# Attention scores as 64-row products, with both softmax maps of a head issued together

## The chip, the cores and the metric

The kernel runs on one core of one Trainium2 chip. The metric is the device time of one execution in microseconds, the median of several runs. Below, PE is the matrix engine (TensorE), PEld its loading of weights, DVE the vector engine, ACT the scalar engine, POOL GpSimd and SP the engine that issues most DMAs.

## The reference, cut to what matters

One layer of a decoder takes 1024 prompt tokens and 8 x 4 sample tokens of width 1024. One input projection feeds a differential attention branch (4 heads) and a state space branch; one output projection adds both to the residual. In the attention, queries and keys are RMS-normed over 64 elements, and each head has two softmax maps:

```python
q = _rmsnorm(q.reshape(b, L, N_HEADS, 2, QK_DIM), q_g)     # QK_DIM = 64
k = _rmsnorm(k.reshape(b, L, N_HEADS, 2, QK_DIM), k_g)
s = jnp.einsum('bqhcd,bkhcd->bhcqk', q, k) * (QK_DIM ** -0.5)   # c: the two maps
s = jnp.where(mask, s + bias, NEG_INF)
p = jax.nn.softmax(s, axis=-1)
w = p[:, :, 0] - lam * p[:, :, 1]
o = jnp.einsum('bhqk,bkhe->bqhe', w, v)
```

The keys (normed) and values of all tokens are outputs too.

## The kernel before, in words

The program has three stages. In the first (about 0 to 240 us) the tokens are loaded and transposed, and the state space branch runs; the order of its PE work is written out by hand. In the second (about 240 to 546 us) `project` computes, head by head and for two tiles of 128 tokens at a time (j = 0 to 3), the head's queries, keys, values and gate. In the third (to the end) `finish` loads the earlier outputs and computes the output projection. The attention of a head (`attention`) runs beside the second and third stage.

In the second and third stage the order is made in two steps. `mix` (line 228) advances several generators in turn: projection, prompt attention and sample attention. Each `yield` names a planned duration, and each stream gets a share of the planned clock. This gives the order of the program text. The tile framework then places each engine's instructions: of those whose inputs and buffers are ready by its own estimate, it takes the one that stands first in the text. So an instruction that isn't ready is passed by later ones, and on the chip each engine runs the order so made.

Float32 operands are split in a high and a low part of type float32r, and products are sums of such parts. In the projections a product is high x high + high x low + low x high, accumulated in one bank of PSUM (`acc`, three buffers).

The part that is changed is this. `keep_qkv` (lines 887 to 912) takes the normed queries and keys of two tiles of tokens, transposes them on PE (line 895, into a buffer `tr`), and writes them to a tile `pt` of 1536 columns. On the 128 partitions the first 64 belong to map 0, the others to map 1. For each map c the high parts of the queries (line 904, ACT) are copied to the other 64 partitions (line 905, DVE), the low parts (line 906, DVE) likewise (line 907, DVE), and the keys of the map get their high parts on partitions 0 to 63 (line 908, ACT) and their low parts on partitions 64 to 127 (line 909, DVE). So one product over all 128 rows gives q x (k high + k low). The keys in float32 (line 910, ACT, tile `kf`) go to the output by a DMA.

`scores` (lines 981 to 1029) handles one block of 128 queries (qb = 0 to 7) against the 128 (qb + 1) keys before it. For each map it goes through segments of up to 512 keys; a segment has one PSUM buffer `sc`, of which there are two. For each 256 keys there are two products (high queries, low queries; lines 1006 and 1007), each with 128 x 128 weights. DVE then reads the segment, adds the bias and takes the minimum (line 1018, one or two instructions to a segment), which frees the buffer. ACT takes the exponential of a map (line 1023), DVE joins both maps (line 1028), and `values` transposes the weights (line 1043) and multiplies them with the values (`pv`). A head has 12 segments to a map. `attn_norm` and `attn_out` (lines 1057 to 1089) norm the result (line 1072, tile `o`) and transpose it (line 1079); the last head's result is written where its queries were in `pt`.

All matrix products go through a helper, line 134, so in the profile they are told apart by their tiles: `acc<-ws,xt` (projection of prompt tokens), `acc<-ws,xs` (of sample tokens, 64 columns of weights), `acc<-ws,o` and `acc<-ws,pt` (output projection), `sc<-pt` (scores), `sc<-cached,qz` (scores of sample tokens, 32 columns of weights), `tr<-cn,qn` (transposes; 32 rows for the sample tokens).

Of the kernel before, what the change touches and what calls it, by code (L numbers as in the profile page):

```python
# [40 lines left out]
# The first phase in its order on the tensor engine: a letter per kind of step, then its index.  # L41
UNITS = ("M0 T0 C20 D0 U0 L0 W N0 M1 P0 C30 X U1 L1 C21 C32 S0 N1 C31 C22 U2 L2 O0 M2 G G U3 S1 G N2 L3 G O1 "
         "M3 G P1 G S2 N3 Q0 G G S3 Z1 G A0 G O2 Z0 B0 Z2 O3 H0 Z3 H1 G H2 G Y0 H3 Y1 Y2 Y3").split()
# Lags of steps of the heads in microseconds, shares of the streams, priorities, numbers of buffers.
# [81 lines left out]
class Kernel:  # L126
# [37 lines left out]
    def load_w(self, src, nk, more=0):  # L164
        """more: the first ones go to tiles of the last phase."""
        nc = self.nc
        w = []
        for kt in range(nk):
            raw = self.raws.tile([128, W], F32, name="wraw", tag="wraw", bufs=3)
            s = src(kt)  # L170
            nc.sync.dma_start(raw.rearrange("p (s c) -> p s c", s=s.shape[1]) if len(s.shape) == 3 else raw, s)
            w.append(self.split_w(raw, kt < more))
        return w
# [11 lines left out]
    def stream_b(self, c0, first=0):  # L185
        """The columns c0.. in halves: a tile holds 256 columns of two row blocks."""
        nc, src = self.nc, self.I["w_in"]
        for half in range(first, 2):
            for k2 in range(KT // 2):
                raw = self.raws.tile([128, W], F32, name="wraw", tag="wraw", bufs=3)  # L190
                c = c0 + 256 * half
                nc.sync.dma_start(raw.rearrange("p (k c) -> p k c", k=2),
                                  src[256 * k2:256 * k2 + 256, c:c + 256].rearrange("(k p) c -> p k c", k=2))
                yield self.split_w(raw)
# [33 lines left out]
    def mix(self, *lanes, until=False):  # L228
        """Emits the pieces of several streams, each getting its share of time; None is a stream that has to wait.
        until: to the end of the first stream only."""  # L230
        lanes = [[g, share, 0.0] for g, share in lanes]
        main = lanes[0]
        while main in lanes if until else lanes:
            for lane in sorted(lanes, key=lambda l: l[2]):
                x = next(lane[0], -1)
                if x == -1:
                    lanes.remove(lane)
                    break
                if x is not None:
                    lane[2] += x / lane[1]  # L240
                    self.clock += x
                    break
            else:
                self.clock += 0.3
            for lane in lanes:
                lane[2] = max(lane[2], main[2] - CAP)
# [9 lines left out]
    def load_x(self, g):  # L256
        """Three tiles of tokens, transposed, as a sum of two parts; their squares summed."""
# [124 lines left out]
    def gate(self, w):  # L382
        """A quarter of twice a silu(): the other gate's tanh() + 1 is twice a sigmoid, too."""
# [52 lines left out]
    # Gate of the state space branch  # L436
# [30 lines left out]
    def glu(self, mo):  # L467
# [5 lines left out]
        # the first one starts before the last inputs are there  # L473
# [27 lines left out]
    def ssm_tables(self):  # L501
# [52 lines left out]
        # the powers of all groups, once for the real and once for the imaginary parts  # L554
# [65 lines left out]
    def ssm_maps(self, m):  # L620
# [4 lines left out]
        # input map of one chunk, states on columns  # L625
# [17 lines left out]
        # output map, real parts of the state above imaginary ones  # L643
# [19 lines left out]
    def ssm_kernel(self, m):  # L663
# [9 lines left out]
        # kernel of one chunk  # L673
# [16 lines left out]
    def ssm_states(self, m):  # L690
# [15 lines left out]
        # recurrence over chunks, turned back by the phase  # L706
# [56 lines left out]
    def lam(self):  # L763
# [18 lines left out]
        # relative bias, negated, over distances  # L782
# [6 lines left out]
    def bias(self):  # L789
# [13 lines left out]
        # of the sample group's rows (batch % 4, -, batch / 4, map, query): distances of the last keys  # L803
        self.bias_rows = lambda h: bass.AP(tensor=d.tensor, offset=row(h) + 127, ap=[[0, 32], [VW, 4], [1, 132]])

    def start_heads(self):
        nc = self.nc
        # one batch's queries, or weights, on the columns of its rows, zeros elsewhere
# [8 lines left out]
    def pt(self, name, dt=F32R):  # L817
        return self.att.tile([128, 1536], dt, name=name, tag="pt", bufs=6)
# [21 lines left out]
    def project(self, w):  # L840
        """The heads' columns for all tokens, into self.heads."""
        nc = self.nc
        due = self.due
        for h in range(NH):
            st = {"ga": {}, "PT": {}, "V": {}, "kept": {}, "out": set()}
            self.heads.append(st)
            for j in range(4):
# [3 lines left out]
                # the last two side by side, so that the weights' tiles get free one after the other  # L851
# [29 lines left out]
    def silu(self, out, x, half_r):  # L881
        """out half_r = silu(2 half_r x)"""
        e = self.small("silu", 128)[0:out.shape[0]]
        self.nc.scalar.activation(e, x, AF.Tanh, scale=half_r)
        self.nc.vector.scalar_tensor_tensor(out, e, 1.0, x, op0=OP.add, op1=OP.mult)

    def keep_qkv(self, h, j, qn, vo, st):
# [10 lines left out]
        half = [slice(64 * c, 64 * c + 64) for c in range(2)]  # L898
        with self.tc.high_priority(HP2):
            # queries of a map twice, one above the other; keys' high parts above their low parts  # L900
            for c, ps in enumerate(half):
                hi, lo, kk = (pt[:, 512 * z + 256 * c:512 * z + 256 * c + 256] for z in range(3))
                ot = half[1 - c]
                nc.scalar.activation(hi[ps], q[ps], AF.Copy, scale=self.gains[ps, 0:1])
                v.tensor_copy(hi[ot], hi[ps].bitcast(F32))  # L905
                v.scalar_tensor_tensor(lo[ps], q[ps], self.gains[ps, 0:1], hi[ps].bitcast(F32), op0=OP.mult, op1=OP.subtract)  # L906
                v.tensor_copy(lo[ot], lo[ps].bitcast(F32))
                nc.scalar.activation(kk[half[0]], k[ps], AF.Copy, scale=self.pkc("k_g")[ps])
                v.scalar_tensor_tensor(kk[half[1]], k[ps], self.pkc("k_g")[ps], kk[half[0]].bitcast(F32), op0=OP.mult, op1=OP.subtract)  # L909
            nc.scalar.activation(kf, k, AF.Copy, scale=self.pkc("k_g"))  # L910
# [19 lines left out]
    def mm_sample(self, a, x, w, kts):  # L930
        """The sample tokens' products, of the high parts in rows 0.. and of the low parts in rows 32.. ."""
# [19 lines left out]
    def attention(self):  # L951
        """The heads' attention in order of projection. The last head's transposed outputs end up where its
        queries were, the others' in DRAM."""
# [27 lines left out]
    def scores(self, h, st_h, qb, job):  # L981
# [9 lines left out]
        st, mn = [], self.small("mn")  # L991
        for c in range(2):
            s = self.big("s")
            st.append(s)
            qh, ql = (PT[j][:, 512 * z + 256 * c + 128 * i:512 * z + 256 * c + 128 * i + 128] for z in (0, 1))
            seg = 0
            last = 3e38
            for k0 in range(0, L, 512):
                kn = min(512, L - k0)
                q = self.sc()  # L1000
                for kk in range(0, kn, 256):
                    n = min(256, kn - kk)
                    pt = PT[(k0 + kk) // 256]
                    k = pt[:, 1024 + 256 * c:1024 + 256 * c + n]
                    o = q[:, kk:kk + n]
                    self.mm(o, qh, k, True, False)
                    self.mm(o, ql, k, False, True)
                far = max(0, min(kn, L - 256 - k0))
                for a0, a1 in ((0, far), (far, kn)):
# [4 lines left out]
                    else:  # L1014
                        x0 = k0 + a0 - (L - 256)
                        bias = job["tb"][:, x0:x0 + a1 - a0]
                    m = mn[:, 4 * c + seg:4 * c + seg + 1]
                    v.tensor_tensor_reduce(out=s[:, k0 + a0:k0 + a1], in0=q[:, a0:a1], in1=bias, op0=OP.add, op1=OP.min,  # L1018
                                           scale=1.0, scalar=last, accum_out=m)
                    last = m  # L1020
                    seg += 1
                yield 0.43 * kn / 512
            nc.scalar.activation(s[:, 0:L], s[:, 0:L], AF.Exp, bias=last, scale=-1.0, accum_out=ls[:, 2 * i + c:2 * i + c + 1])  # L1023
# [68 lines left out]
    def cached(self, src):  # L1092
        """A batch's two pages of cached keys or values of one head."""
# [8 lines left out]
    def sample_attend(self):  # L1102
        """The sample group's attention, head by head. Rows: (batch % 4, -, batch / 4, map, query)."""
# [90 lines left out]
    def reload(self, c0, n):  # L1194
        """Tokens of the branches' outputs, but the last head's, as a sum of two parts."""
# [59 lines left out]
    def split_s(self):  # L1255
        """The sample group's part of the state space branch."""
# [23 lines left out]
def _arrays(x):  # L1280
# [10 lines left out]
    def turned(v):  # L1291
        """The state space branch's channels, (block, group, channel), in the order (block, channel, group)."""
# [76 lines left out]
```

## Time and profile before

| | us |
|---|---|
| runs before: median (lowest to highest of 3) | 679.38 (678.92 to 679.74) |
| span of the profiled execution, first to last instruction | 678.4 |
| PE busy (weights: PEld) | 608.0 (502.2) |
| DVE / ACT / POOL busy | 483.9 / 313.1 / 159.8 |

The profile is of one execution; the page gives its span, and no other time of it. Busy times are sums over the whole span; the ends of matrix products are modelled and overlap their successors, so the pace of products is better read from how many there are in a stretch. The chain of waits is followed back from the last instruction.

### The profile page before, as it was taken

The numbers are of one execution on the slowest core, as the hardware profiler recorded it, in microseconds if no ns is written. First come the engines' busy times: TensorE is split into PE (matmuls) and PEld (weight loads), VectorE is DVE, ScalarE is ACT, GpSimd is POOL, SyncE is SP. The second block draws the span as 40 slices with busy tenths as digits, with TensorE's granted clock in tenths as the row PEclk, the third lists the DMA queues.
The fourth block names the chain that finished last, engine by engine and source line by source line (L and its number), as shares of the span: only waits on it lengthen the run. The fifth ranks groups of instructions, "written<-read, shape, count | busy, mean of one in ns | idle before, by whom it ended". The sixth has DMA issues, their size and how long they took to land.

```text
span 678.4 us, 11431 instructions
## 1 busy us (share of the span) xinstructions
PE 608.0 (90%) x3562; PEld 502.2 (74%) x3562; DVE 483.9 (71%) x1639; ACT 313.1 (46%) x984; POOL 159.8 (24%) x165
## 2 busy tenths in 40 slices
PE   5797849778787999989999899998999989999997
PEld 4786839677676887768877688776887767886775
DVE  3888997899764437799677996689966898832111
ACT  5772322122273326676456764567645677412000
POOL 0473679677524400030000300003000020001100
PEclk9997978897988999999999999999999998999999
DMA  8223608252255450153001530025300166333221
GB/s 329 83 71 112 138 18 217 65 153 73 82 187 168 163 170 16 55 146 112 24 23 55 148 110 25 23 58 149 105 16 31 56 190 207 122 107 125 81 83 50
DMA packets 82474, 70.31 MB, mean 104 GB/s; under 512 B 8493, under 2 KB 71502, under 8 KB 82414
## 3 DMA queue, kind: packets, MB, share of 16 engines
q1 hardware_dynamic: 80110, 65.18, 32.3%
q10 hardware_dynamic: 2304, 4.41, 1.8%
q8 instruction: 28, 0.46, 0.3%
q14 instruction: 32, 0.26, 0.1%
HBM read 49.52 MB, written 20.04 MB: 103 GB/s over the span
## 4 chain that ended last, share of the span: by engine, by line
PE 48%; DVE 30%; ACT 8%; DMA 5%; issue 5%; POOL 3%; SPq 1%; POOLq 0%; ACTq 0%; DVEq 0%
PE acc L134 32%; PE sc L134 5%; PE pv L134 4%; DVE s L1018 3%; PE tr L1043 2%; DVE ws L182 2%; PE tr L134 2%; DVE pt L906 1%; DMA zr<-zd 1%; DVE pt L909 1%; DMA wraw<-in_w_out 1%; DVE et L495 1%; ACT ws L179 1%; DVE E_re L496 1%; DVE pt L905 1%
## 5 line engine op out<-in xcount | busy, mean ns | idle before, releaser
L134 PE MATMUL acc<-ws,xt 128*128 128x512 f32 x768 | 204.6, 403 | 0.4 <-DVE gz L489 0.4
L134 PEld LDWEIGHTS acc<-ws,xt 128*128 128x128 f32 x768 | 137.1, 189 | 25.9 <-issue 1.2
L182 POOL TENSOR_TENSOR ws<-wraw,ws 128x512 fp32r<-128x512 f32 x30 | 47.6, 1591 | 365.3 <-ACT ws L179 217.6
L134 PE MATMUL acc<-xt,ws 128*128 128x352 f32 x576 | 100.6, 332 | 0.8 <-ACT xt L266 0.8
L134 PEld LDWEIGHTS acc<-xt,ws 128*128 128x128 f32 x576 | 94.7, 193 | 3.0 <-issue 1.2
L134 PE MATMUL acc<-ws,o 128*128 128x512 f32 x336 | 84.6, 400 | 3.3 <-ACT ws L179 1.5
L134 PEld LDWEIGHTS acc<-ws,o 128*128 128x128 f32 x336 | 63.3, 192 | 17.7 <-ACT ws L179 2.0
L1023 ACT ACTIVATE s<-s,mn 128x128 f32<-128x128 f32 (+7 forms) x64 | 49.7, 778 | 28.4 <-DVE mn L1018 18.6
L134 PE MATMUL sc<-pt 128*128 128x256 f32 (+1 forms) x320 | 57.9, 296 | 5.1 <-DVE mn L1018 2.6
L134 PEld LDWEIGHTS sc<-pt 128*128 128x128 f32 x320 | 46.0, 189 | 21.7 <-DVE mn L1018 5.2
L179 ACT ACTIVATE ws<-wraw 128x512 fp32r<-128x512 f32 x68 | 41.7, 628 | 33.1 <-PE acc L134 22.6
L1252 DVE TENSOR_TENSOR xres<-acc,xres 128x512 f32<-128x512 f32 x16 | 11.0, 690 | 51.9 <-PE acc L134 51.9
L134 PE MATMUL pv<-vo,wt 128*128 128x128 f32 x288 | 41.9, 284 | 0.0
L134 PEld LDWEIGHTS pv<-vo,wt 128*128 128x128 f32 x288 | 37.9, 196 | 4.0 <-ACT wt L1046 1.9
L182 DVE TENSOR_TENSOR ws<-wraw,ws 128x512 fp32r<-128x512 f32 x38 | 29.3, 782 | 5.1 <-ACT ws L179 5.1
L134 PE MATMUL acc<-z,ws 128*128 128x352 f32 x144 | 26.5, 342 | 5.1 <-DVE gs L394 1.9
L134 PEld LDWEIGHTS acc<-z,ws 128*128 128x128 f32 x144 | 24.7, 199 | 6.8 <-DVE gs L394 2.5
L393 ACT ACTIVATE acc<-gs 128x352 f32<-128x352 f32 x12 | 5.6, 468 | 51.1 <-DVE gs L392 49.6
L1043 PE MATMUL tr<-cn,s 128*128 128x128 f32 x144 | 26.8, 278 | 1.2 <-ACT kf L910 1.2
L828 ACT ACTIVATE qn<-acc 128x64 f32<-128x64 f32 x128 | 26.9, 227 | 0.0
L1018 DVE CUSTOM_DVE_ANT_0 s<-sc,cb 128x512 f32<-128x512 f32 (+3 forms) x48 | 26.3, 549 | 0.5
L1028 DVE SCALAR_TENSOR_TENSOR s<-s,ls 128x128 f32<-128x128 f32 (+7 forms) x32 | 26.0, 813 | 0.3
(287 smaller groups left out, 1109.5 us busy)
## 6 DMA issues: line engine op xcount, KB each, us to landing
wraw<-in_w_in SPq DMA_DIRECT2D x44, 256.0 KB, 3.1
xtok<-in_x SPq DMA_DIRECT2D x8, 512.0 KB, 9.2
cached<-in_cache_k SPq DMA_DIRECT2D x64, 64.0 KB, 1.9
cached<-in_cache_v SPq DMA_DIRECT2D x64, 64.0 KB, 1.9
wraw<-in_w_out SPq DMA_DIRECT2D x16, 256.0 KB, 3.2
xres<-in_x SPq DMA_DIRECT2D x16, 256.0 KB, 2.9
out_y<-xres SPq DMA_DIRECT2D x16, 256.0 KB, 2.0
ud<-uT SPq DMA_DIRECT2D x4, 580.0 KB, 5.7
```

Source lines behind the costliest of these rows:

```text
L134: self.nc.tensor.matmul(out, lhsT, rhs, start=start, stop=stop)
L179: nc.scalar.activation(hi, raw, AF.Copy)
L182: (nc.vector if self.turn else nc.gpsimd).tensor_tensor(lo, raw, hi.bitcast(F32), op=OP.subtract)
L495: eng.tensor_tensor(t1, a_im, b_im, op=OP.mult)
L496: eng.tensor_tensor(o_re, o_re, t1, op=OP.subtract)
L828: nc.scalar.activation(qn[0:n, i, 64 * c:64 * c + 64], a[0:n, 64 * c:64 * c + 64], AF.Square, accum_out=ss[0:n, 4 * i + c:4 * i + c + 1])
L905: v.tensor_copy(hi[ot], hi[ps].bitcast(F32))
L1018: v.tensor_tensor_reduce(out=s[:, k0 + a0:k0 + a1], in0=q[:, a0:a1], in1=bias, op0=OP.add, op1=OP.min, scale=1.0, scalar=last, accum_out=m)
L1023: nc.scalar.activation(s[:, 0:L], s[:, 0:L], AF.Exp, bias=last, scale=-1.0, accum_out=ls[:, 2 * i + c:2 * i + c + 1])
L1028: v.scalar_tensor_tensor(wv, st[1][:, 0:L], cf, wv, op0=OP.mult, op1=OP.add)
L1043: nc.tensor.transpose(q[:, 128 * b:128 * b + 128], wv[:, 128 * (b0 + b):128 * (b0 + b) + 128], self.idn)
L1252: v.tensor_tensor(x, a, x, op=OP.add)
```

## The change: what it does

Queries and keys of a map stay on the map's own 64 partitions. `pt` holds only the queries, 256 columns of high parts and 256 of low parts for both maps (512 columns instead of 1536, still six buffers). A new tile `kk` holds the keys of four token tiles, 512 columns of high and 512 of low parts (three buffers). The copies to the other half are gone, and each of the remaining instructions treats all 128 partitions. In `scores` the two maps advance together, segment by segment: both take a PSUM buffer, and for each of the three products (high x high, high x low, low x high) map 0 is multiplied on rows 0 to 63 and map 1 on rows 64 to 127, over up to 512 keys. DVE's reading of the two buffers follows, and both exponentials come after the last segment. The planned time of a segment of 512 keys is 0.72 for both maps, where it was 0.43 for each. Comments were removed as well. No DMA is added or removed.

```diff
     def pt(self, name, dt=F32R):
-        return self.att.tile([128, 1536], dt, name=name, tag="pt", bufs=6)
+        return self.att.tile([128, 512], dt, name=name, tag="pt", bufs=6)
@@ keep_qkv
-        half = [slice(64 * c, 64 * c + 64) for c in range(2)]
+        if j % 2 == 0:
+            st["K"][j // 2] = self.att.tile([128, 2, 512], F32R, name="kk", tag="kk", bufs=3)
+        kh, kl = (st["K"][j // 2][:, z, 256 * (j % 2):256 * (j % 2) + 256] for z in range(2))
+        qh, ql = pt[:, 0:256], pt[:, 256:512]
+        kg = self.pkc("k_g")
         with self.tc.high_priority(HP2):
-            for c, ps in enumerate(half):
-                hi, lo, kk = (pt[:, 512 * z + 256 * c:512 * z + 256 * c + 256] for z in range(3))
-                ot = half[1 - c]
-                nc.scalar.activation(hi[ps], q[ps], AF.Copy, scale=self.gains[ps, 0:1])
-                v.tensor_copy(hi[ot], hi[ps].bitcast(F32))
-                v.scalar_tensor_tensor(lo[ps], q[ps], self.gains[ps, 0:1], hi[ps].bitcast(F32), op0=OP.mult, op1=OP.subtract)
-                v.tensor_copy(lo[ot], lo[ps].bitcast(F32))
-                nc.scalar.activation(kk[half[0]], k[ps], AF.Copy, scale=self.pkc("k_g")[ps])
-                v.scalar_tensor_tensor(kk[half[1]], k[ps], self.pkc("k_g")[ps], kk[half[0]].bitcast(F32), op0=OP.mult, op1=OP.subtract)
-            nc.scalar.activation(kf, k, AF.Copy, scale=self.pkc("k_g"))
+            nc.scalar.activation(qh, q, AF.Copy, scale=self.gains[:, 0:1])
+            v.scalar_tensor_tensor(ql, q, self.gains[:, 0:1], qh.bitcast(F32), op0=OP.mult, op1=OP.subtract)
+            nc.scalar.activation(kh, k, AF.Copy, scale=kg)
+            v.scalar_tensor_tensor(kl, k, kg, kh.bitcast(F32), op0=OP.mult, op1=OP.subtract)
+            nc.scalar.activation(kf, k, AF.Copy, scale=kg)
@@ scores
-        for c in range(2):
-            s = self.big("s")
...
-            for k0 in range(0, L, 512):
-                kn = min(512, L - k0)
-                q = self.sc()
-                for kk in range(0, kn, 256):
...
-                    self.mm(o, qh, k, True, False)
-                    self.mm(o, ql, k, False, True)
+        for k0 in range(0, L, 512):
+            kn = min(512, L - k0)
+            kh, kl = (st_h["K"][k0 // 512][:, z, 0:kn] for z in range(2))
+            qs = [self.sc() for c in range(2)]
+            for n, (x, y) in enumerate(((qh, kh), (qh, kl), (ql, kh))):
+                for c, ps in enumerate(half):
+                    self.mm(qs[c][:, 0:kn], x[ps], y[ps], n == 0, n == 2)
+            far = max(0, min(kn, L - 256 - k0))
+            for c in range(2):
+                s, q = st[c], qs[c]
...
-                yield 0.43 * kn / 512
-            nc.scalar.activation(s[:, 0:L], s[:, 0:L], AF.Exp, bias=last, scale=-1.0, accum_out=ls[:, 2 * i + c:2 * i + c + 1])
+            yield 0.72 * kn / 512
+        for c in range(2):
+            s = st[c]
+            nc.scalar.activation(s[:, 0:L], s[:, 0:L], AF.Exp, bias=last[c], scale=-1.0, accum_out=ls[:, 2 * i + c:2 * i + c + 1])
```

## Rows read from the trace of the kernel before

**Rows 1.** Stretches: busy us of PE, PEld, DVE, ACT, POOL (counts), granted clock, DMA.

```profile
338.00:423.00 85.00, 82.31 (x502) 64.50 (x501) 68.85 (x308) 51.13 (x191) 5.92 (x4) 1.00 0.25 72
546.00:600.00 54.00, 49.84 (x294) 40.39 (x293) 45.53 (x175) 33.85 (x99) 5.46 (x4) 0.94 0.56 172
```

**Rows 2.** The page's chain of waits over the whole span, by engine.

```profile
PE 48%; DVE 30%; ACT 8%; DMA 5%; issue 5%; POOL 3%; SPq 1%; POOLq 0%; ACTq 0%; DVEq 0%
```

**Rows 3.** Chain of waits from 402 to 410 us: start, us, what.

```profile
403.15 0.95 PE sc L134 x8
...
405.50 4.17 PE acc L134 x18
```

**Rows 4.** Groups by form, 240 to 600 us: busy us, mean ns | idle before.

```profile
L134 PE MATMUL sc<-pt 128*128 128x256 f32 x256 | 47.3, 301 | 4.0 <-DVE mn L1018 2.6 <-DVE qr L161 0.7 <-DVE pt L905 0.6
...
L909 DVE SCALAR_TENSOR_TENSOR pt<-tr,pk,pt 64x256 fp32r<-64x256 f32 x32 | 15.5, 484 | 5.2 <-ACT pt L908 4.6
...
L908 ACT ACTIVATE pt<-tr,pk 64x256 fp32r<-64x256 f32 x32 | 15.0, 470 | 21.7 <-DVE pt L906 21.6
...
L905 DVE CAST pt<-pt 64x256 fp32r<-64x256 f32 x32 | 9.2, 289 | 14.0 <-ACT pt L904 13.6
...
L1087 DVE SCALAR_TENSOR_TENSOR pt<-tr,gains,pt 128x256 fp32r<-128x256 f32 x3 | 1.4, 475 | 0.2 <-ACT pt L1086 0.2
```

**Rows 5.** Timeline of PE from 280 us, 32-column weights: start, us, what, count.

```profile
280.75 1.07 PE L134 MATMUL sc<-cached,qz 128*32 128x256 f32 x16
281.64 0.31 PE L134 MATMUL sc<-ks,qz 128*32 128x32 f32 x16
```

**Rows 6.** Timeline of PE and PEld from 277.2 us, around two 32-row products.

```profile
277.22 1.09 PE L134 MATMUL acc<-ws,xt 128*128 128x512 f32 x4
278.24 0.31 PE L941 MATMUL tr<-cn,qn 32*128 32x32 f32 x2
278.47 1.20 PE L134 MATMUL acc<-ws,xt 128*128 128x512 f32 x4
...
277.22 0.65 PEld L134 LDWEIGHTS acc<-ws,xt 128*128 128x128 f32 x3
278.24 0.20 PEld L941 LDWEIGHTS tr<-cn,qn 32*128 32x128 f32 x2 [0.37 <-issue]
```

**Rows 7.** Timeline of PE and DVE from 316 us, in a burst of scores.

```profile
317.44 0.74 PE L134 MATMUL sc<-pt 128*128 128x256 f32 x4
...
316.68 0.69 DVE L1018 CUSTOM_DVE_ANT_0 s<-sc,cb 128x512 f32<-128x512 f32 x1
...
317.92 0.48 DVE L1018 CUSTOM_DVE_ANT_0 s<-sc,TB,mn 128x256 f32<-128x256 f32 x1
```

**Rows 8.** Timeline of PE from 287.9 us: one segment in two pieces.

```profile
287.90 0.39 PE L134 MATMUL sc<-pt 128*128 128x256 f32 x1
...
288.82 0.54 PE L134 MATMUL sc<-pt 128*128 128x256 f32 x3
```

**Rows 9.** Waits from 240 to 600 us: total us, times, longest.

```profile
PE tr L1079 <- DVE o L1072: 3.4, 7, 0.7
PE sc L134 <- DVE mn L1018: 2.8, 5, 0.8
...
PEld sc L134 <- DVE mn L1018: 6.5, 11, 1.3
...
PEld sc L134 <- DVE pt L909: 3.9, 13, 0.6
```

**Rows 10.** Timeline of PE and PEld at 269 us: after 64-column weights of type float32r.

```profile
268.63 1.08 PE L134 MATMUL acc<-ws,xs 128*64 128x512 f32 x4
269.55 0.74 PE L134 MATMUL sc<-pt 128*128 128x256 f32 x5
...
269.32 0.77 PEld L134 LDWEIGHTS sc<-pt 128*128 128x128 f32 x5
```

More of the change, by code (lines that the diff above doesn't have):

```diff
@@ L844, in project @@
         for h in range(NH):
-            st = {"ga": {}, "PT": {}, "V": {}, "kept": {}, "out": set()}
+            st = {"ga": {}, "PT": {}, "K": {}, "V": {}, "kept": {}, "out": set()}
             self.heads.append(st)
@@ L990, in scores @@
         L = 128 * nb
-        st, mn = [], self.small("mn")
-        for c in range(2):
-            s = self.big("s")
[L994 to L997, printed above, removed]
-            for k0 in range(0, L, 512):
-                kn = min(512, L - k0)
-                q = self.sc()
-                for kk in range(0, kn, 256):
[L1002 to L1005, printed above, removed]
-                    self.mm(o, qh, k, True, False)
-                    self.mm(o, ql, k, False, True)
-                far = max(0, min(kn, L - 256 - k0))
+        st, mn = [self.big("s") for c in range(2)], self.small("mn")
+        half = [slice(64 * c, 64 * c + 64) for c in range(2)]
+        qh, ql = (PT[j][:, 256 * z + 128 * i:256 * z + 128 * i + 128] for z in range(2))
+        segs, last = [0, 0], [3e38, 3e38]
+        for k0 in range(0, L, 512):
[8 more added lines that the diff above has]
+                s, q = st[c], qs[c]
                 for a0, a1 in ((0, far), (far, kn)):
@@ L1016, in scores @@
                         bias = job["tb"][:, x0:x0 + a1 - a0]
-                    m = mn[:, 4 * c + seg:4 * c + seg + 1]
+                    m = mn[:, 4 * c + segs[c]:4 * c + segs[c] + 1]
                     v.tensor_tensor_reduce(out=s[:, k0 + a0:k0 + a1], in0=q[:, a0:a1], in1=bias, op0=OP.add, op1=OP.min,
-                                           scale=1.0, scalar=last, accum_out=m)
-                    last = m
-                    seg += 1
-                yield 0.43 * kn / 512
-            nc.scalar.activation(s[:, 0:L], s[:, 0:L], AF.Exp, bias=last, scale=-1.0, accum_out=ls[:, 2 * i + c:2 * i + c + 1])
+                                           scale=1.0, scalar=last[c], accum_out=m)
+                    last[c] = m
+                    segs[c] += 1
+            yield 0.72 * kn / 512
+        for c in range(2):
+            s = st[c]
+            nc.scalar.activation(s[:, 0:L], s[:, 0:L], AF.Exp, bias=last[c], scale=-1.0, accum_out=ls[:, 2 * i + c:2 * i + c + 1])
         cf = ls[:, 4 + i:5 + i]
```

## The prediction, made before the changed kernel ran

> **What bounds the kernel now.** I read the busy times in stretches first. In the stretch of one head PE is busy 82.31 of 85.00 us, DVE 68.85, ACT 51.13, and the granted clock is 1.00, that is 2.4 GHz [rows 1]. So PE sets the time while the attention runs, and DVE is the engine next to it. The stretch at the end of the attention is alike, with PE at 49.84 of 54. The page's chain of waits then shows where PE is not limited by its own work: 48% of it is PE, but 30% DVE [rows 2]. The reader should see there that two things count: the time that PE's own products take, and the times at which PE stands at the head of its queue and waits for DVE. The first stage and the output projection hold nothing that the change touches, and no DMA, nor anything on the queues of SP and POOL, is added or removed.
>
> **The pace of products.** In the chain eight score products of 256 columns take 0.95 us, 0.119 each, and eighteen projection products of 512 columns take 4.17, 0.232 each [rows 3]. The difference, 0.113 for 256 columns, is 0.441 ns a column, with 6 ns to each product. The means of the groups (301 ns for a score product [rows 4]) are the time through the array and overlap; they are not the pace.
>
> **Products removed.** Each head and map has 20 pieces of up to 256 keys with two products each: 320 products, of which 256 have 256 columns [rows 4] and 64 have 128. At 0.119 each that is 38.1 us at most (the 64 short ones cannot take longer than the long ones).
>
> **Products added.** A head has 12 segments, together 4608 columns to a map. Three products on each of two maps give 6 x 4608 x 4 heads = 110,592 columns in 288 products. One after the other they take 110,592 x 0.441 ns + 288 x 6 ns = 50.5 us; if the two maps run side by side all the time, half, 25.2. No two products on different rows stand together in the trace. The nearest row is the sample scores, whose weights take 32 columns: 16 products of 256 columns start within 0.89 us (280.75 to 281.64), 0.056 each, less than half of the 0.119 of a full product of that length [rows 5]. So products on different parts of the array do run together. I take it that halves by rows do so too, where both are there to be issued.
>
> Whether both are there is the planner's matter. The framework takes the first ready instruction in the order of the text. The evidence is a segment in two pieces: one score product, then 0.9 us later the other three, with transposes and projection products between [rows 8]. In a burst the score buffers are what a segment waits for: DVE's reading ends at 317.37, and the next score products start at 317.44 [rows 7]. With both maps in one segment, the buffer of map 0 comes free first and that of map 1 only after its own readings (0.69 and 0.48 for a long segment [rows 7]). When map 0's is free, its first product is ready, then its second and third (they need the same buffer and operands that have long been there), while map 1's are not. So in such a segment I expect three products of map 0 alone and those of map 1 behind them, nearly in series. The segments that begin anew after a wait for new queries (4 of 12 in a head, 1536 of 4608 columns) find both buffers free and run side by side. For the other 8 I take 5.5 steps of 6, as the last product of map 0 and the first of map 1 can overlap. Sum: a third of 25.2, 8.4, and two thirds of 50.5 x 5.5 / 6, 30.9; together 39.3 us. The bounds are 25.2 and 50.5.
>
> **Changing the shape of the array.** Weights of 64 rows stand among products with 128 rows. The trace has the like with 32 rows [rows 6]. Four projection products start at 277.22 and are through at 277.22 + 4 x 0.232 = 278.15. The weights of the small product start at 278.24, 0.09 later, where the weights of the rows before start together with the running product. The projection comes back at 278.47, and its next four products take 1.20 where the four before took 1.09: 0.11 more, as weights are loaded with nothing running. So the work goes on as from 278.58. The visit cost 0.43, of which the two small products stream some 0.03. I take 0.40 for each visit to 64 rows. Before, scores had the shape of all else and such visits were free. With 48 segments there are at least 48 visits, 19.2 us; with every one of the 32 waiting segments in two pieces there are 80, 32.0. I take 60, nearer the lower end since map 1's buffer often comes free within the 0.7 us that map 0's three products last: 24.0 us.
>
> The Trainium skill, "TensorE: Matmul & The Clock Gate", in the section on packing small matmuls, says that weights are loaded beside running products only where the row groups differ. The rows show otherwise: weights of 128 rows start with the running products of the same rows [rows 6]. By the page's rule the next weights of a map could not load under its own product, and with 0.11 uncovered in each of 144 pairs the sum below would be some 16 us higher; I leave that out.
>
> **DVE and ACT.** For each of 32 halves the copies (0.289 twice) and the low parts (0.484 twice) go: lines 905 and 907 are alike, 9.2 us each, 906 and 909 too, 15.5 each [rows 4]. That is 49.4 us of DVE. What comes is 32 instructions over 128 partitions and 256 columns, 0.475 each by the nearest row, 15.2. DVE is relieved of 34.2 us, about 8.5 of 69 in a head's stretch. ACT loses 32 of the 64 instructions of lines 904 and 908 (15.0 us each), 15.0 us. None of it is on the path as such; what counts is PE's waits. The rows show waits for DVE of 2.8 (score buffers) and 3.4 (normed outputs) at the products and 6.5 and 3.9 (score buffers and keys) at their weights [rows 9]; the last two are partly covered by a running product. Together 16.6. The path to the first score shortens from ACT and DVE in turn for two maps to ACT, ACT. The upper bound is that all of it goes, the lower is zero, if PE meets the same waits in other places. As the queue of DVE is shorter everywhere, I take 14.0. What is late next is the reading of the score buffers itself, which does not get shorter.
>
> **Waits added.** A segment now needs both buffers. Behind a waiting score product on PE stand projection products, so a wait that the planner did not foresee stops everything. In the rows such waits are 0.5 us in the mean (2.8 in five [rows 9]); I leave them within the 14.0. The exponential of map 0 comes after both maps' segments instead of before map 1's; ACT has 34 of 85 us free [rows 1], so I take nothing, and at most one exponential of a block, about 1 us, at the last head's end.
>
> **Sum.** 39.3 - 38.1 + 24.0 - 14.0 = +11.2 on the profile's 678.4. Its span lies 1.0 below the median of the runs, so 690.6 for the median. Its own range, with 48 to 80 visits (-4.8, +8.0) and the relief between 8 and 17, is 683 to 700.
>
> **Rivals.**
> First, the planner leaves the six products together, because it sees both buffers free when their turn comes. Speaks for it: many score runs are whole [rows 7]. Against: the cut segment [rows 8]. Then 25.2 - 38.1 + 19.2 - 14.0 = -7.7: 671.7, faster. It decides from where fewer than about a quarter of the waiting segments are cut.
>
> Second, changing to 64 rows costs nothing. For it: weights of 64 columns of type float32r are followed by full ones with no loss. The fourth of four products starts at 269.32, the next weights start at 269.32, and the next product at 269.55 [rows 10]; the scores are float32r too, and the 32-row case is float32 [rows 6]. Then 39.3 - 38.1 - 14.0 = -12.8: 666.6. It decides from a visit below 0.2 us. The Trainium skill, "TensorEngine Tiling (Array Packing)", in the key properties, says that any change of tiling mode drains the engine; rows 6 agree and rows 10 do not.
>
> Third, halves of rows do not run together, but the shape changes: 50.5 - 38.1 + 24.0 - 14.0 = +22.4: 701.8. For it: nothing in the trace shows two products on different rows at once; against, the columns [rows 5].
>
> Fourth, the change does not do what it says: 64-row products pass as full ones, one after the other, with no change of shape. 50.5 - 38.1 - 14.0 = -1.6: 677.8. Rows 10 speak for that as well.
>
> **How the numbers follow.** Forecast 0.50, first rival 0.14, second 0.11, third 0.14, fourth 0.11. A difference of 0.2%, 1.4 us, is about what the runs can tell from none. Faster: 0.11 of the first, 0.11 of the second, 0.06 of the fourth, 0.04 of the forecast's tail, 0.32. Same: 0.03 of the forecast, 0.02 of the first, 0.03 of the fourth, 0.08. Slower: 0.60. The range runs from 667 (half of the second rival below it) to 704 (half of the third above it); about 0.15 is left out.
>
> **What the new profile would show.** The forecast is right if 64-row weights start some 0.1 us after the last full product is through, the four projection products after them take about 1.2 us, and score runs number near 60 with many of three products of one map. Products of both maps starting within some 10 ns show side by side; 0.23 apart at 512 columns show series. The relief shows in shorter waits of PE for DVE than in rows 9. The forecast is wrong if runs of six are the rule (first rival), if the next full weights start with the last score product (second), or if the pairs start 0.2 apart everywhere (third and fourth, told apart by the visits).

## The result and the profile after

The changed kernel takes 683.95 us (median of six runs, 682.88 to 685.99), the kernel before 679.15 (six, 677.23 to 681.21): ratio 1.0081, 95% interval 1.0063 to 1.0098. It is slower, as forecast, but by 4.8 us instead of 11.2. The profiled execution of the changed kernel is the slowest of its six (685.99, span 684.2), that of before an ordinary one (679.38, span 678.4). So the two traces differ by 5.8 us in their spans, and some 2 us of what the changed kernel's trace shows belong to that one execution.

The same two stretches as in [rows 1]; then the chain by engine, which answers to [rows 2].

```profile
338.00:423.00 85.00, 83.67 (x494) 62.20 (x493) 60.83 (x280) 47.99 (x182) 5.78 (x4) 1.00 0.25 72
546.00:600.00 54.00, 50.94 (x268) 36.57 (x267) 41.24 (x149) 32.01 (x91) 5.11 (x4) 0.94 0.54 168
```

```profile
PE 61%; DVE 20%; DMA 7%; ACT 4%; issue 3%; POOL 3%; SPq 1%; POOLq 0%; DVEq 0%; ACTq 0%
```

DVE lost 8.0 us of its 68.9 in a head's stretch (8.5 were forecast) and went from 30% to 20% of the chain, PE from 48% to 61%. Yet heads 1 and 2 last 84.27 us from first projection product to first projection product in both traces. What PE gained by not waiting it spent on something else.

The groups by form of the changed kernel, 240 to 600 us, for [rows 4], and the waits of PE and PEld in that stretch, for [rows 9] (total us, times, longest):

```profile
L134 PE MATMUL sc<-kk,pt 64*128 64x512 f32 x144 | 31.4, 432 | 0.0
...
L906 DVE SCALAR_TENSOR_TENSOR pt<-tr,gains,pt 128x256 fp32r<-128x256 f32 x16 | 7.7, 482 | 11.2 <-ACT pt L905 11.2
...
L908 DVE SCALAR_TENSOR_TENSOR kk<-tr,pk,kk 128x256 fp32r<-128x256 f32 x16 | 7.7, 482 | 6.1 <-ACT kk L907 6.1
```

```profile
PE tr L1178 <- DVE ob L1175: 3.4, 3, 1.2
PE acc L134 <- ACT o L1202: 3.0, 1, 3.0
...
PE sc L134 <- DVE mn L1014: 0.4, 1, 0.4
PE tr L1077 <- DVE o L1070: 0.2, 1, 0.2
...
PEld sc L134 <- DVE mn L1014: 2.5, 7, 0.7
```

The waits that the forecast wanted gone are mostly gone: score products wait 0.4 for their buffers (2.8 before) and their weights 2.5 (6.5 before), the transposes of normed outputs 0.2 (3.4 before). Two others are the largest now: transposes wait 3.4 for the sample group's `ob`, and one product of the output projection stands 3.0 for ACT. Now one visit to the 64-row products and the cut one after it, on PE (start, us, what, count), and the weights of the same stretch on PEld:

```profile
317.56 0.98 PE L134 MATMUL sc<-kk,pt 64*128 64x512 f32 x6
318.46 0.96 PE L134 MATMUL acc<-ws,xt 128*128 128x512 f32 x3
319.35 0.96 PE L134 MATMUL sc<-kk,pt 64*128 64x512 f32 x3
320.24 0.49 PE L134 MATMUL acc<-ws,xt 128*128 128x512 f32 x1
```

```profile
317.55 0.54 PEld L134 LDWEIGHTS sc<-kk,pt 64*128 64x128 f32 x6
318.46 0.53 PEld L134 LDWEIGHTS acc<-ws,xt 128*128 128x128 f32 x3 [0.37 <-issue]
```

Six products of 512 columns take 0.90 us until the projection goes on, and three of one map also 0.89: the six run as three pairs. Within them the two maps' products start 3 ns apart (317.896 and 317.899), the next pair 0.24 later. The weights on both sides of a visit start only when the products of the other shape are through: the last pair starts at 318.14, its 512 columns last some 0.21, and the projection's weights start at 318.46. So they are loaded with nothing running.

**A ledger of PE.** From the first projection product of head 0 to the last product of the kernel, I split the time between the starts of following products (where a product and its weights start together, the weights' time is taken off first): columns at 2.4 a ns and 4 ns a product, the rest is a gap, put down to the two products around it. Visits are the runs of score products in PE's order of instructions. Each row is of one execution, the profiled one. How much time the weights are given is a convention: with 0.107 us, the distance between two loads in the visit above, the changed kernel's gaps into and out of visits become 15.6 and 14.0 and its last column 382.0. So differences of 1 to 2 us between the columns of a row mean little.

```
us                  whole  visits  score    gaps between  gaps into  gaps out    all
                                   columns  score prod.   a visit    of a visit  else
before              439.2    86     32.0        6.5         15.1        1.7     383.9
after               446.0    64     33.1        2.3         14.0       12.7     383.9
e1_full_rows        438.7    64     47.2        5.0          4.9        1.3     380.2
e8_same_half        457.8    64     47.2        4.6         13.8       12.3     379.9
e2_before_light     428.1    77     32.0        4.1          8.6        1.4     382.0
e3_dve_put_back     466.8    85     35.8        5.2         21.9       20.1     383.8
e4_early_wout       442.1    64     33.1        2.1         13.3       12.3     381.2
e6_copies_pool      433.9    90     32.0        5.1         14.0        1.7     381.0
e5_whole_visits     446.7    51     24.9        2.6         19.0       10.7     389.6
e9_bias_first       442.7    51     24.9        1.8         17.8        9.8     388.5
e12_bias_on_pool    437.8    51     24.9        1.8         10.4        9.8     391.0
```

### The profile page after: what moved, and what is told of

The parts are those of the page before. It is cut to its first block, busy times and chain, and to the rows that moved or that the text cites. A ratio compares the mean times of both kernels' runs of the same rounds, so it can differ in the third digit from the quotient of the medians.

```text
span 684.2 us, 11236 instructions
## 1 busy us (share of the span) xinstructions
PE 619.4 (91%) x3530; PEld 495.4 (72%) x3530; DVE 456.4 (67%) x1543; ACT 300.3 (44%) x952; POOL 158.5 (23%) x165
## 4 chain that ended last, share of the span: by engine, by line
PE 61%; DVE 20%; DMA 7%; ACT 4%; issue 3%; POOL 3%; SPq 1%; POOLq 0%; DVEq 0%; ACTq 0%
PE acc L134 42%; PE sc L134 8%; PE pv L134 5%; PE tr L1041 2%; PE tr L134 2%; DVE ws L182 1%; DMA xtok<-in_x 1%; DMA wraw<-in_w_out 1%; POOL gz L465 1%; PE tr L895 1%; DVE E_re L496 1%; DVE E_re L494 1%; DMA zd<-Z 1%; DVE et L495 1%; DVE X L720 1%
## 5 line engine op out<-in xcount | busy, mean ns | idle before, releaser
L179 ACT ACTIVATE ws<-wraw 128x512 fp32r<-128x512 f32 x68 | 41.6, 629 | 38.6 <-PE acc L134 25.5
L134 PE MATMUL sc<-kk,pt 64*128 64x512 f32 (+3 forms) x288 | 53.1, 379 | 0.4 <-DVE mn L1014 0.4
L134 PEld LDWEIGHTS sc<-kk,pt 64*128 64x128 f32 x288 | 30.6, 187 | 20.3 <-issue 5.9
L182 DVE TENSOR_TENSOR ws<-wraw,ws 128x512 fp32r<-128x512 f32 x38 | 34.9, 934 | 7.8 <-ACT ws L179 7.3
L134 PEld LDWEIGHTS acc<-z,ws 128*128 128x128 f32 x144 | 25.5, 206 | 5.3 <-DVE gs L394 4.3
L1044 ACT ACTIVATE wt<-tr 128x512 f32<-128x512 f32 (+3 forms) x48 | 23.0, 490 | 8.8 <-PE tr L1041 8.7
```

The source lines that it names most:

```text
L134: self.nc.tensor.matmul(out, lhsT, rhs, start=start, stop=stop)
L179: nc.scalar.activation(hi, raw, AF.Copy)
L182: (nc.vector if self.turn else nc.gpsimd).tensor_tensor(lo, raw, hi.bitcast(F32), op=OP.subtract)
L1044: nc.scalar.activation(wt[:, 0:128 * bn], q[:, 0:128 * bn], AF.Copy)
```

## The experiments

**No change of shape** (every product over 128 rows).

```
-  self.mm(qs[c][:, 0:kn], x[ps], y[ps], n == 0, n == 2)
+  self.mm(qs[c][:, 0:kn], x, y, n == 0, n == 2)
```

> The changed kernel with the six products of a visit taken over all 128 rows instead of 64 (the two maps' scores are then mixed: their separation is left out). Same instructions in the same order on every engine; no product has another shape than the projection's, and no two can run side by side. Theory (a visit of the 64-row products costs 0.41 us in changes of shape, 64 visits; whole pairs run side by side, so the six products of 512 columns stream in some 0.7 us instead of 1.44): the changes go, -26 us, and the streaming goes from some 35 to some 50 us, +15: about 11 us faster than the changed kernel, 673 us (668 to 678). Rival (the change of shape costs next to nothing, the side by side running carries the time): +15 us, about 699 us.

Measured: 679.74 us, ratio to before 1.0026 (1.0003 to 1.0050), so about 4 us faster than the changed kernel. The direction is the theory's, the size is not. In the ledger the gaps into and out of visits fall by 20.5 us, which is 64 visits at 0.32 (they were 0.42 each, but an ordinary hand-off costs some 0.1 too, 6.2 in 64 visits here), and columns and gaps between score products rise by 16.8. The rival is dead: the change of shape is not free. A visit of six in this kernel, on PE:

```profile
316.36 1.65 PE L134 MATMUL sc<-kk,pt 128*128 128x512 f32 x6
317.85 0.86 PE L134 MATMUL acc<-ws,xt 128*128 128x512 f32 x3
318.57 0.96 PE L134 MATMUL sc<-kk,pt 128*128 128x512 f32 x3
```

A visit of six takes 1.49 us instead of 0.90 until the projection goes on, but the three projection products behind it take 0.72 and the three products of one map 0.80, instead of 0.89 each. A whole visit gains by the new form and a cut one loses.

**The same shape, but both maps in one half.**

```
-  self.mm(qs[c][:, 0:kn], x[ps], y[ps], n == 0, n == 2)
+  self.mm(qs[c][:, 0:kn], x[half[0]], y[half[0]], n == 0, n == 2)
```

> The changed kernel with both maps' products taken from partitions 0 to 63: the same shapes, order and number of instructions, but no two products on different rows (map 1's scores are then map 0's). Ledger theory (side by side running halves the streaming of the pairs): the 64 changes of shape stay, the streaming rises from 33 to 47 us: 14 us slower than the changed kernel, 694 to 700 us. Rival (the pairs' gain comes from hidden weight loads and would be there in one half too): within 4 us of the changed kernel, 682 to 688 us.

Measured: 700.18 us, ratio 1.0316 (1.0277 to 1.0356), as the ledger theory expects at its upper end. Columns rise by 14.1, and the gaps at the visits' ends stay (26.1 for 26.7). (The ledger's whole rises by 11.8 only, since its last column is 4.0 lower; the medians differ by 16.) So the pairs run at once because they stand on different rows. The same visit on PE:

```profile
323.37 1.65 PE L134 MATMUL sc<-kk,pt 64*128 64x512 f32 x6
324.95 0.96 PE L134 MATMUL acc<-ws,xt 128*128 128x512 f32 x3
```

**The lighter preparation in the kernel before.**

```
-  for c, ps in enumerate(half):      # per map, on 64 rows: ACT high part, DVE copy,
-      ...                            # DVE low part, DVE copy, ACT and DVE for the keys
+  nc.scalar.activation(qh, q, AF.Copy, scale=self.gains[:, 0:1])
+  v.scalar_tensor_tensor(ql, q, self.gains[:, 0:1], qh.bitcast(F32), ...)
+  nc.scalar.activation(kh, k, AF.Copy, scale=kg)
+  v.scalar_tensor_tensor(kl, k, kg, kh.bitcast(F32), ...)
```

> The kernel before with the changed kernel's queries' and keys' preparation (two ACT copies, two DVE subtractions over 128 rows, no copies to the other half), its products and their order of issue by maps as they were (both maps read the same rows; their separation is left out). Theory (what the changed kernel gained back, some 24 us in heads 0 to 2 and 3, is the lighter DVE work, which made the tensor engine wait before score products): some 15 to 25 us faster than the kernel before, 655 to 664 us. Rival (the gain came from the scores being issued for both maps at once, which gives each buffer more time): within 3 us of the kernel before, 676 to 682.

Measured: 669.49 us, ratio 0.9861 (0.9838 to 0.9884): 9 us, where I expected 15 to 25. Gaps into visits fall by 6.5 and those between score products by 2.4. The expectation came from a first reading of the two traces, which put the relief at 24 us because heads 0 to 2 take equally long; the ledger corrects it.

**The heavier preparation in the changed kernel** (each conversion in two pieces of 64 rows, and behind it, for the queries):

```
+  v.tensor_copy(xh[ot], qh[ps].bitcast(F32))
...
+  v.tensor_copy(xl[ot], ql[ps].bitcast(F32))
```

> The changed kernel with the kernel before's work in the preparation put back: per call, each conversion in two pieces of 64 rows and four DVE copies of 64x256, here into columns that nothing reads. Theory (the DVE work is what was gained): 14 to 24 us slower than the changed kernel, 698 to 708 us. Rival (issue by both maps at once was the gain): within 3 us of the changed kernel, 682 to 687.

Measured: 706.21 us, ratio 1.0426 (1.0398 to 1.0454), as expected, but by another way than I had thought. The planner, with DVE later everywhere, cuts the scores into 85 visits instead of 64. Gaps into and out of visits rise by 15.3 us, columns by 2.7 and gaps between score products by 2.9. So in this kernel the load of the preparation decides how often the shape changes. ACT's conversions are in pieces here too, and no run separates them from DVE's.

**The first tile of the output weights earlier.** In head 3 of the changed kernel's profiled execution SP's issues, then ACT, then PE, and the clock in two stretches (columns as in [rows 1]):

```profile
470.92 6.49 SPq L1094 DMA_DIRECT2D cached<-in_cache_k  x11
...
478.00 1.39 SPq L171 DMA_DIRECT2D wraw<-in_w_out  x3
```

```profile
482.33 0.63 ACT L179 ACTIVATE ws<-wraw 128x512 fp32r<-128x512 f32 x1 [1.86 <-DMA wraw<-in_w_out]
```

```profile
483.87 0.44 PE L1041 MATMUL tr<-cn,s 128*128 128x128 f32 x2 [1.15 <-ACT wt L1044]
```

```profile
482.00:486.00 4.00, 2.42 (x12) 1.34 (x11) 2.70 (x9) 2.23 (x5) 0.00 (x0) 1.00 0.32 97
486.00:490.00 4.00, 4.00 (x17) 3.24 (x19) 1.34 (x7) 2.93 (x10) 0.00 (x0) 0.57 0.07 24
```

ACT stands (waits) 1.86 us on a tile that SP issued behind 16 cached keys (5 more stand ahead of the 11 shown), PE stands behind ACT, and the granted clock falls after it.

```
-  nc.sync.dma_start(raw ..., s)
+  (nc.gpsimd if first and kt == 0 else nc.sync).dma_start(raw ..., s)
```

> The changed kernel with the first tile of the output projection's weights fetched through POOL's queue, where no cached keys stand before it. Theory (the 5 us that the changed kernel lost against the one before all arose in head 3, where ACT stood 1.9 us on that transfer, the tensor engine after it, and the granted clock fell to 0.57): 4 to 5 us faster than the changed kernel, 679 to 680 us. Rival (the loss is a steady cost of the visits which only shows there): within 1 us of the changed kernel, 683 to 685.

Measured: 682.72 us, ratio 1.0064 (1.0048 to 1.0080), 1.2 us better than the changed kernel; the two intervals overlap, so this is about as much as the runs can tell from nothing. In its trace the stand is gone, the next stretch runs at clock 1.00, and its ledger is 3.9 shorter:

```profile
486.00:490.00 4.00, 4.00 (x24) 2.63 (x22) 2.39 (x14) 3.11 (x16) 0.00 (x0) 1.00 0.02 4
```

So in the median of six the stand is worth about a quarter of the loss at most, and my 4 to 5 us had been read from the slowest execution.

**Whole visits.** Edges for the planner: the first product waits for DVE's last reading of both old buffers, the other five are ordered behind it.

```
+  for r in (self.read if n == c == 0 else (first,)):
+      self.tc.add_manual_dep(m, r.name, ...)
```

> The changed kernel with edges for the planner: the first product of a visit waits for DVE's last reading of both buffers of the visit before, and the other five come behind it. 51 visits instead of 64, 46 of them with the six products in pairs (29 before). Ledger theory (the 64 visits cost 0.32 us each over ordinary hand-offs, products in pairs stream in half the time): streaming and gaps between score products from 35.4 to some 26 us, changes from 20.5 to 16.3: -13 us, less new waits for the second buffer of 0 to 8 us: 671 to 679 us, most likely 674. Rival (the planner's split was what kept the tensor engine from waiting for DVE; whole visits bring back waits as the kernel before had them): no gain, 683 to 690 us.

Measured: 683.95 us, ratio 1.0079 (1.0049 to 1.0110): nothing gained. The columns fell from 33.1 to 24.9 and the gaps out of visits by 2.0, as expected, and all of it was given back. DVE, then PE, at one place of this kernel, and the clock around it:

```profile
382.73 0.19 DVE L1122 TENSOR_TENSOR sbias<-cn,sbias 128x32 f32<-128x32 f32 x1 [4.13 <-DMA sbias<-tbd]
382.84 0.68 DVE L1020 CUSTOM_DVE_ANT_0 s<-sc,cb 128x512 f32<-128x512 f32 x1
```

```profile
384.33 1.01 PE L1001 MATMUL sc<-kk,pt 64*128 64x256 f32 x6 [3.37 <-DVE mn L1020]
```

```profile
380.00:390.00 10.00, 6.63 (x50) 4.18 (x49) 7.06 (x30) 4.62 (x17) 2.55 (x2) 0.67 0.30 86
```

DVE stands 4.13 us on the sample group's bias, in front of the reading that the next visit waits for. That happens once in each of heads 0 to 2. (This trace is of the slowest of its nine executions.) Is it whole visits as such, or that one instruction? First the earlier output weights were added:

> The kernel with whole visits and the first tile of the output projection's weights fetched through POOL's queue: both edits together. Theory (the edits are independent): 1 us faster than with whole visits alone. Rival (the stall on that tile was hidden): the same within 0.5 us.

Measured: 683.57 us, ratio 1.0077 (1.0047 to 1.0107), 0.4 us less. That is nearer to the rival, but the intervals are too wide to tell it from the theory. Then, on top of both, the bias's transfer was issued first:

```
-  keys = [self.cached(...) for b in range(NB)]
   bias = self.att.tile([128, 164], F32, name="sbias", tag="sbias", bufs=1)
   nc.sync.dma_start(bias[:, 0:132], self.bias_rows(h))
+  keys = [self.cached(...) for b in range(NB)]
```

> Whole visits, the first output weights through POOL's queue, and the sample group's bias fetched ahead of the 16 cached keys on SP's queue instead of behind them. Theory (whole visits gained 8.2 us of streaming and 2 us of changes; what ate it was no wait for the second buffer as such, but DVE standing 4 us per head on the bias, L1122, in front of one reading, which held a visit for 2.6 to 3.4 us in three heads, and the slower granted clock after each): the three waits of together 9 us go, and the clock stays up: 669 to 676 us, most likely 673. Rival (the wait belongs to whole visits and moves to another instruction): 681 to 685 us.

Measured: 683.90 us, ratio 1.0087 (1.0062 to 1.0111). The edit missed its aim. SP's issues, then DVE, of this kernel, then PE's waits for that reading, 240 to 580 us, and the clock behind the stand:

```profile
368.14 5.91 SPq L1101 DMA_DIRECT2D cached<-in_cache_v  x11
...
375.11 0.54 SPq L1118 DMA_DIRECT2D sbias<-tbd  x1
```

```profile
379.46 0.19 DVE L1122 TENSOR_TENSOR sbias<-cn,sbias 128x32 f32<-128x32 f32 x1 [3.41 <-DMA sbias<-tbd]
```

```profile
PE sc L1001 <- DVE mn L1020: 7.2, 3, 2.7
```

```profile
380.00:385.00 5.00, 3.95 (x48) 2.85 (x49) 5.00 (x20) 2.62 (x7) 1.32 (x1) 1.00 0.23 66
```

The bias now stands ahead of the keys, but the cached values are still ahead of both, and DVE stands as before; PE loses 7.2 us by it in three waits. In this trace the clock stays at 1.00 behind them. So the instruction itself was moved off DVE:

```
-  v.tensor_tensor(new..., op=OP.add)      # L1122
+  g.tensor_tensor(new..., op=OP.add)
```

> The kernel of whole visits with the bias first, and the one addition L1122 moved from DVE to POOL; the order of instructions on the tensor engine is the same. Fetching the bias first left DVE standing 3.4 us on it in heads 0 to 2, since its transfer is issued late all the same. Theory (that instruction, and not whole visits as such, holds the three visits of 2.6 to 3.2 us): the three waits go, 8.6 us, and with them the slower clock behind: 670 to 676 us. Rival (another instruction takes the place of L1122, since DVE reads the buffers late anyway): 681 to 684 us.

Measured: 676.09 us, ratio 0.9971 (0.9952 to 0.9990), the theory's upper end. PE's order of instructions is that of the run before; one addition of 0.2 us a head on another engine is worth 8 us. The same addition, now on POOL, and PE's waits, 240 to 580 us, in this kernel:

```profile
378.17 0.24 POOL L1122 TENSOR_TENSOR sbias<-cn,sbias 128x32 f32<-128x32 f32 x1 [7.61 <-DVE mn L1020]
```

```profile
PE tr L1084 <- DVE o L1077: 6.3, 4, 2.0
PE tr L1185 <- DVE ob L1182: 3.9, 3, 1.4
PE sc L134 <- DVE mn L1020: 1.4, 2, 0.8
```

The three waits of 7.2 for DVE's reading are gone; two others, 1.4, are left. POOL is idle for 7.61 us before the addition. Its row names DVE, and not the transfer, as what ended that, so it does not show how long the bias itself was late. The gaps into visits are down to 10.4 for 51 visits, 0.20 each, which is the bare price of entry. Some 7 us of what whole visits gain still go into the rest of PE's time (all else 391.0 against 383.9). The largest waits there are the two for transposes, 6.3 and 3.9; the run before has them too, with 4.8 and 4.0.

**Parts of the change alone, on the kernel before.** The four copies on POOL:

```
-  v.tensor_copy(hi[ot], hi[ps].bitcast(F32))
+  g.tensor_copy(hi[ot], hi[ps].bitcast(F32))      # and the same for lo
```

> The kernel before with its four copies of queries to the other half on POOL instead of DVE; nothing else. Theory (DVE's work ahead of the score products is what the tensor engine waits for; taking 34 us off DVE was worth 9 us, so 18 us are worth about 5): 673 to 676 us. Rival (POOL's slower copies end later than DVE's did, and the score products wait for them): 679 us or more.

Measured: 674.46 us, ratio 0.9940 (0.9918 to 0.9962), as the theory has it, and the lowest median of all kernels here that compute the whole result. The copies take longer there (groups by form, 303 to 387 us of this kernel; 289 ns on DVE in [rows 4]), and little waits for them:

```profile
L905 POOL CAST pt<-pt 64x256 fp32r<-64x256 f32 x8 | 3.4, 423 | 59.2 <-ACT pt L904 59.2
...
L907 POOL CAST pt<-pt 64x256 fp32r<-64x256 f32 x8 | 3.2, 397 | 2.1 <-DVE pt L906 1.1 <-DVE s L159 0.5
```

The order of issue (the loops over segments and maps exchanged), alone and with the copies on POOL:

```
-  for c in range(2):
-      for k0 in range(0, L, 512):
+  for k0 in range(0, L, 512):
+      for c in range(2):
```

> The kernel before with the changed kernel's order of issue alone: a segment of map 0, then the same segment of map 1, and both exponentials behind them; products, shapes and preparation as they were. Theory (what the tensor engine no longer waits ahead of the scores comes from DVE's lighter preparation): within 2 us of the kernel before, 677 to 681. Rival (it comes from the order of issue, which gives each buffer more time to be read): 668 to 674 us.

> The kernel before with its four copies on POOL and the changed kernel's order of issue. Theory (order of issue is worth little): within 2 us of the copies on POOL alone, 673 to 677 us. Rival (with the copies off DVE, the order decides): 667 to 671 us.

Measured: 676.20 us, ratio 0.9971 (0.9953 to 0.9988), and 675.77, ratio 0.9957 (0.9939 to 0.9974). The order alone is worth some 2 us (678.80 before in the same session), 0.8 us beyond what the theory allowed and 2.2 short of the rival; on top of the copies it adds nothing.

## Why the prediction was right in direction and wrong in size

**What failed is the step on products added**: "for the other 8 I take 5.5 steps of 6". It sized the term at 39.3 us; the ledger has 33.1 of columns and 2.3 of gaps, 35.4. In series they would have been 52.2 (e1), whole visits 26.7 (e9 and e12), so the planner kept 66% of what pairing can give ((52.2 - 35.4) / 25.5) where my working kept 44% ((50.5 - 39.3) / 25.3). In PE's order 29 of the 64 visits hold all six products of a segment in pairs; I had looked for 16 of 48 segments. That segments are cut as in [rows 8] was right; that nearly all waiting ones would run in series was not. Nor did the series come in the form that the working gave it, map 1 behind map 0 in one visit: where a pair broke, it made two visits, and 27 of the 64 have three products. Why so many pairs held is only argued: with DVE relieved, the planner finds map 1's buffer free when map 0's is. The heavier preparation, with its 85 visits, fits that.

**Products removed**: 38.1 forecast, 38.5 in the ledger (32.0 + 6.5). That they agree is partly luck. The working charged the 64 short products as long ones, and the 6.5 of gaps hold waits for DVE, which belong to the relief: with the lighter preparation and the same products the gaps are 4.1.

**Shape**: 60 visits at 0.40, 24.0, were forecast; 64 at 0.42 came, but 0.32 over an ordinary hand-off, 20.5. The working had called the visits before free, and e1 shows that they cost 0.1 each. The price read from a float32 visit of 32 rows [rows 6] held for 64 rows of float32r; that weights of 64 columns cost nothing [rows 10] did not carry over. The Trainium skill's "TensorEngine Tiling (Array Packing)", key properties, says that a change of tiling mode drains the engine, and gives no price. The visits here agree, with the 0.32 over an ordinary hand-off.

**Relief**: 14.0 forecast. By e1, which has the changed kernel's order without its shapes, the gaps at visits fell from 16.8 to 6.2, 10.6; some 2 us of that are the ordinary hand-offs of 22 fewer visits and no waits. The two terms were both too large by about 3.5, and that they cancel is luck: +10.0 forecast, +9.9 in the ledger (26.7 - 16.8). How the two divide hangs on the ledger's convention (with 0.107 us to the weights they are 23.3 and 11.5); the products' 35.4 hardly does (34.5).

**The sum** in the ledger is 35.4 - 38.5 + 20.5 - 10.6 = +6.8, for +11.2. The rest of the kernel is even (383.9 twice), though not by nothing happening: some 3 us go with the stand on the output weights in head 3 (e4 has 381.2), against waits that are gone elsewhere. Head 1 alone, where both kernels need 84.27: shape +4.8, relief -3.4, products -1.3. The span shows 5.8, since head 0 began 1.0 earlier, and the medians 4.8. That the sum came out on the slow side hung on the pairs that broke: with whole visits, two transfers moved and the addition off DVE it is 2 us on the fast side. In the working's own range the upper end adds up to 704.6 (690.6 + 8.0 + 6.0), not 700.

**Waits added** were looked for in PE's queue and not in ACT's. The tile of w_out in head 3 is a wait that the new order put in front of the copy of transposed weights, for which PE waits. It costs at most 1.2 us in the median. A second one was taken at nothing as well: the product of the output projection that stands 3.0 us for ACT (line 1202, which splits earlier outputs that are loaded again). Before, the like waits were 0.5 for ACT and 0.7 for DVE, and e4 keeps it at 2.9. No run takes it away, so its price is open.

**The rivals** can each be priced by a kernel that is that case. First, whole visits: 671.7 forecast, 676.1 measured, and only after one addition had left DVE. Third, halves in series: 701.8, measured 700.2 (e8). Fourth, no change of shape: 677.8, measured 679.7 (e1). The second, a free change, has no kernel; e1 excludes it. To count on weights that load beside products of the same rows, as [rows 6] shows, was right: six products with six loads take 0.90 us. The packing section of the Trainium skill's "TensorE: Matmul & The Clock Gate" says that they do so only where the row groups differ, and this trace does not agree.

**Not settled** is what of e12's other waits belongs to its order, and why the clock falls after a stand in one execution and not in the next: whole visits stand 2.31, 3.37 and 2.13 us before three visits, in stretches of 10 us at clock 0.83, 0.67 and 0.83, while with the bias first the same three stands, 2.37, 2.66 and 2.14, have 1.00. That bears on the spread of single executions, 3 us for the changed kernel and 7 for whole visits: of whole visits the slowest (688.21) has a mean granted clock of 0.940, the fastest (680.78) 0.962.

## What to carry to other kernels

When a product's shape differs from its neighbours', count the visits before the columns: a visit costs 0.4 us here and pairing six products of 512 columns saves 0.7 (0.90 against 1.58), so the gain hangs on the planner's keeping pairs whole. In this kernel an instruction that waits for a late transfer belongs on an engine on which nothing urgent is queued behind it. And price one stage's terms by a kernel in the same order with one property taken away; a period that stays the same may hide terms of 3 to 5 us that cancel.

## What was not expected of the hardware

Two float32r products on rows 0 to 63 and 64 to 127, to different PSUM buffers, start 3 ns apart and take the time of one; in one half they follow each other (0.90 against 1.58 us for six). The way into 64-row products costs some 0.2 us and the way out some 0.2, ordinary hand-off included, for the 27 visits of three products as for the 33 of six. After 4 us in which PE was busy for 2.42, the granted clock was 0.57 in the next 4 us (changed kernel); it was 0.67 over a stretch of 10 us that holds a stand of 3.37 (whole visits). That is, partly at 1.2 GHz instead of 2.4, so a stand can cost more than its length. It need not: with the bias first, a stand of 2.66 us of the same visit was followed by 1.00.
